# Another order of experts by slot count in a single-core decoder trunk, with gathering groups of three and four

## The chip, the cores and the metric

One Trainium2 chip, of which the kernel uses one core. The metric is the device time of one execution in microseconds (us), the median over runs. In the text PE is TensorE (PEld its weight loads), DVE is VectorE, ACT is ScalarE, POOL is GpSimd and SP is SyncE, which here issues the weight loads.

## The reference, cut to what matters

Two decoder layers on 256 tokens of width 1024. Layer 0 is a state-space mixer and a dense SwiGLU, layer 1 a dilated attention and then a top-2-of-8 mixture of experts, with a LayerNorm behind each. Only the mixture is touched here:

```
logits = x @ w_router
top_v, top_i = lax.top_k(logits, TOP_K)                 # 2 of 8 experts for each token
gates = jax.nn.softmax(top_v, axis=-1)
...
for e in range(N_EXPERTS):
    y = _swiglu(x, w1[e], w3[e], w2[e])                 # (silu(x @ w1) * (x @ w3)) @ w2, inner width 3584
    out = out + gate_full[..., e, None] * y
```

Everything is float32. The weights of one expert are 44.04 MB (42 pieces of 1 MiB).

## The kernel before, in words

**Slots.** An expert computes only the tokens that chose it. They are gathered into a fixed number of slots, 96 or 64 (`CAPS`, L35). `RANKS` (L34) is the order of use: expert 0 comes first whatever its count, and position i of the others takes the expert of rank `RANKS[i]`, where rank 0 is the expert with the most tokens. Ranks 0 to 3 have 96 slots, ranks 4 to 6 have 64. `places()` and `order()` work the ranks out on the chip, and SP loads the seven addresses of the weights into registers. Expert 0 has 96 slots too, but a branch (L1526) takes a path of 64 slots when at most 64 tokens chose it; the trace shows that path (28 of the 56 multiplications of L1453 have 256 columns, the others 384). In what follows e0 to e7 are the positions of use. Before, their slots are 64, 64, 96, 64, 96, 96, 96, 64, with e0 counted as it ran.

**Chunks.** Each expert has 7 chunks of 512 inner columns. A chunk takes six loads of 1 MiB: four for `up` (w1 and w3) and two for `down` (w2). `chunks()` runs on PE, in order of program: the first halves of `up` of chunk n, the transposes (`flip`) of chunk n-1, two pieces of side work (`aside`), `up` again, then `down` of chunk n-1. A 64-slot expert needs one pass over each load, with two column tiles of 64. A 96-slot expert needs a second pass over the same load (`rest` and `down(n, 1)`) with four column tiles of 32. After the last `down` of an expert, L1579 copies its result out of PSUM (`yw`), and the scatter back to the tokens (`scatter`, L1435) runs as side work in the next expert. So the start of L1579 on DVE is used as the border between experts.

**The ring.** All weight loads go through one queue, SP's, into a ring of 17 buffers of 1 MiB (`Stream`). A load is issued in order as soon as the next buffer has been given back (`give`): behind the only pass of a 64-slot expert, behind the second pass of a 96-slot expert. PE waits for a load with its first matmul on it. The order of loads is fixed.

**Gathering.** The tokens of several experts are gathered together (`GROUPS`, L37): `gather(g)` is eight steps, each four matmuls of as many columns as the group has slots, and a copy to `xe`. Group 0 is expert 0. `gather(1)` runs all at once between e0 and e1, with nothing else on PE. `gather(2)` is side work from the second chunk of e2 on, two steps in a chunk. `one_hots` (L1208) makes the matrices that it multiplies by.

Of the kernel before, what the change touches and what calls it, by code (L numbers as in the profile page):

```python
# [30 lines left out]
PIECES = 6 * NJ  # L31


RANKS = (7, 4, 0, 5, 1, 2, 3, 6)  # L34
CAPS = tuple(96 if i == 0 or r < 4 else 64 for i, r in enumerate(RANKS))  # L35

GROUPS = ((0,), (1, 2, 3, 4), (5, 6, 7))  # L37
SLOTS = max(sum(CAPS[i] for i in g) for g in GROUPS)


# [110 lines left out]
def trunk(ctx: ExitStack, tc: tile.TileContext, a, out, dbg=None):  # L151
# [839 lines left out]
    with ExitStack() as e:  # L991
# [212 lines left out]
        def one_hots(g, src=by_i):  # L1204
            c = 0
            for i in GROUPS[g]:
                for t in range(2):
# [114 lines left out]
    OTg = mw.tile([128, 2, 128], F32, name="OTg")  # L1322
    xes = [mw.tile([128, 8, sum(CAPS[i] for i in g)], F32, name=f"xe{g[0]}") for g in GROUPS[1:]]

# [5 lines left out]
    def experts(ws, pas, pyy):  # L1330
        if pas:
            V.tensor_tensor(out=by_i[:, 2:4, :], in0=by_i[:, 2:4, :], in1=cst[:, None, 24:32].to_broadcast([128, 2, 8]), op=S_)
        with ExitStack() as e:
# [18 lines left out]
            def gather(g):  # L1352

                c, x_, o_ = sum(CAPS[i] for i in GROUPS[g]), xes[g], Ob
                nk = 1 if g else 2
# [35 lines left out]
            def up(n, i, b):  # L1391

                ee = n // NJ
                g = [q for q in range(3) if ee in GROUPS[q]][0]
                x_, x0 = xes[g], sum(CAPS[q] for q in GROUPS[g] if q < ee)
                if b == 0:
# [223 lines left out]
def _constants():  # L1620
# [20 lines left out]
    e = np.arange(8)  # L1641
    uni[:, 392:424] = np.concatenate([PIECES * e, 7 - e, RANKS, CAPS])
    ident = np.zeros((128, 160), np.float32)
# [82 lines left out]
```

## Time and profile before

| | us |
|---|---|
| median of 3 runs | 1506.89 (1505.99 to 1507.74) |
| profiled execution, its own time | 1505.6 |
| its span, first to last instruction | 1503.8 |
| PE busy | 1431.1 (95%) |
| DVE busy | 534.7 (36%) |
| ACT busy | 384.0 (26%) |
| expert part, e1 to e7, by L1579 (start of e1's part 750.06, end of e7 1485.83) | 735.8 |

The busy time of PE covers the whole span; matmuls are pipelined, so a busy PE may still wait a little inside. HBM moved 458.31 MB, of which 334 loads of the expert weights of 1 MiB each are listed as one group.

### The profile page before, as it was taken

How to read it: one execution, taken by the hardware profiler on the slowest of the kernel's cores; microseconds unless marked ns; L12 is line 12 of the kernel's file. 1: busy time of each engine (PE TensorE's matmuls, PEld its weight loads, DVE VectorE, ACT ScalarE, POOL GpSimd, SP SyncE). 2: the span in 40 equal slices, each digit the busy share in tenths (PEclk: the TensorE clock that was granted, in tenths of full speed). 3: DMA queues.
4: the chain of work that ended last, by engine and by line, in shares of the span. 5: the costliest groups of instructions: out<-in, count | busy, mean ns of one | idle time of the engine just before them, and what ended most of it. 6: DMA issues, size and time to landing. Idle time of an engine off the chain costs nothing. (4 is left out here: it accounts for less than half of the span.)

```text
span 1503.8 us, 32304 instructions
## 1 busy us (share of the span) xinstructions
PE 1431.1 (95%) x14108; PEld 1040.5 (69%) x14108; DVE 534.7 (36%) x1022; ACT 384.0 (26%) x633; POOL 125.9 (8%) x162
## 2 busy tenths in 40 slices
PE   7869999999999999999998899998999999999996
PEld 6658899998999999865554466654556665666552
DVE  9998745446666655550110110110100100100103
ACT  6535544334554545420110000100000100100100
POOL 0110566001021000001000000000000000000001
PEclk9889999999999999989999999999999999999998
DMA  7007488554445544459999999999999999999995
GB/s 260 7 30 301 174 258 262 192 182 186 148 154 199 180 154 171 172 242 424 425 426 426 426 425 425 425 425 427 425 424 426 417 397 401 363 372 393 406 426 212
DMA packets 68412, 458.31 MB, mean 305 GB/s; under 512 B 9041, under 2 KB 9716, under 8 KB 15780
## 3 DMA queue, kind: packets, MB, share of 16 engines
q1 hardware_dynamic: 62896, 444.68, 73.5%
q0 software_dynamic: 4128, 8.87, 2.2%
q10 hardware_dynamic: 1236, 2.58, 0.5%
q8 instruction: 115, 1.88, 0.5%
q14 instruction: 37, 0.30, 0.1%
HBM read 454.97 MB, written 3.48 MB: 305 GB/s over the span
## 5 line engine op out<-in xcount | busy, mean ns | idle before, releaser
L1384 PE MATMUL a<-raw,xe 128*64 128x256 f32 (+1 forms) x7152 | 514.1, 328 | 8.5 <-DMA raw<-in_moe 7.8
L1384 PEld LDWEIGHTS a<-raw,xe 128*64 128x64 f32 (+1 forms) x7152 | 349.4, 124 | 162.8 <-issue 24.8
L1384 PE MATMUL y<-raw,h 128*32 128x256 f32 (+1 forms) x1792 | 255.7, 488 | 7.0 <-DMA raw<-in_moe 6.0
L1453 DVE TENSOR_TENSOR sl<-sl,a 128x256 f32<-128x256 f32 (+1 forms) x56 | 27.3, 488 | 562.8 <-PE a L1384 562.6
L110 DVE TENSOR_TENSOR sp<-raw,sp 128x2048 fp32r<-128x2048 f32 (+1 forms) x84 | 187.9, 2243 | 98.3 <-ACT sp L109 98.3
L1384 PEld LDWEIGHTS y<-raw,h 128*32 128x32 f32 (+1 forms) x1792 | 89.9, 123 | 151.5 <-issue 118.9
L109 ACT CAST sp<-raw 128x2048 fp32r<-128x2048 f32 (+1 forms) x85 | 154.3, 1823 | 68.7 <-PE ab L928 32.8
L1103 PE MATMUL qkp<-xT,sp 128*128 128x256 f32 x1152 | 153.1, 287 | 0.0
L1451 ACT ACTIVATE sl<-a 128x256 f32<-128x256 f32 (+1 forms) x56 | 24.5, 438 | 501.4 <-PE a L1384 501.3
L1103 PEld LDWEIGHTS qkp<-xT,sp 128*128 128x128 f32 x1152 | 141.9, 191 | 1.9
L928 PE MATMUL ab<-xT,sp 128*128 128x256 f32 x960 | 117.0, 283 | 0.0
L928 PEld LDWEIGHTS ab<-xT,sp 128*128 128x128 f32 x960 | 116.5, 192 | 0.7
L759 POOL TENSOR_TENSOR lr__1387<-lr__1387,mhalf 128x1 f32<-128x1 f32 x8 | 4.5, 568 | 855.4 <-DVE lr__1387 L758 855.4
L972 PE MATMUL pv<-sp,xT 128*128 128x384 f32 x384 | 72.3, 343 | 3.3 <-ACT xT L800 3.3
L972 PEld LDWEIGHTS pv<-sp,xT 128*128 128x128 f32 x384 | 67.4, 192 | 5.0 <-ACT xT L800 3.8
L1413 ACT COPY h<-ht 128x256 f32<-128x256 f32 (+1 forms) x56 | 23.8, 426 | 181.5 <-PE ht L1412 180.4
L916 PE MATMUL facc<-sp,hh 128*128 128x512 f32 x176 | 54.5, 390 | 0.0
L692 PE MATMUL glu<-sp,xT 128*128 128x512 f32 x144 | 36.7, 415 | 4.3 <-DVE sp L110 4.3
L1436 DVE SCALAR_TENSOR_TENSOR xx<-so,by_i,xx 128x512 f32<-128x512 f32 x28 | 19.7, 746 | 57.6 <-PE so L1435 57.6
L474 PE MATMUL pu<-x0T,raw 128*128 128x256 f32 x128 | 30.7, 403 | 8.3 <-DMA raw<-in_w_in 8.3
L692 PEld LDWEIGHTS glu<-sp,xT 128*128 128x128 f32 x144 | 28.7, 201 | 11.7 <-DVE sp L110 5.1
L916 PEld LDWEIGHTS facc<-sp,hh 128*128 128x128 f32 x176 | 32.4, 188 | 6.3
(270 smaller groups left out, 1164.9 us busy)
## 6 DMA issues: line engine op xcount, KB each, us to landing
raw<-in_moe SPq DMA_DIRECT2D x334, 1024.0 KB, 19.4
raw<-in_ffn SPq DMA_DIRECT2D x33, 1024.0 KB, 6.1
raw<-in_qk SPq DMA_DIRECT2D x24, 1024.0 KB, 4.8
raw<-in_wv SPq DMA_DIRECT2D x16, 768.0 KB, 4.4
raw<-in_w_glu SPq DMA_DIRECT2D x8, 1024.0 KB, 4.7
raw<-in_w_o SPq DMA_DIRECT2D x4, 1024.0 KB, 4.7
raw<-in_w_in SPq DMA_DIRECT2D x3, 1024.0 KB, 10.4
skew<-vecs POOLq DMA_DIRECT2D x64, 36.0 KB, 4.1
```

Source lines behind the costliest of these rows:

```text
L109: self.nc.scalar.copy(out=h_, in_=t_)
L110: (eng or self.nc.vector).tensor_tensor(out=l_, in0=t_, in1=h_, op=ALU.subtract)
L474: T.matmul(pu[:, mm].rearrange("p a b -> p (a b)"), lhsT=w[:, k, mm * 128:mm * 128 + 128], rhs=x0T[:, k, :], start=(k == 0 and mm == mms[0 ...
L692: T.matmul(o[t], lhsT=s_, rhs=m_, start=(kk == 0 and i == 0), stop=(kk == 7 and i == 2))
L916: T.matmul(acc[t][n], lhsT=s_, rhs=m_, start=(j == 0 and f == 0 and ip == 0), stop=(j == NFP - 1 and f == 1 and ip == 2))
L928: T.matmul(o[:, f, :], lhsT=s_, rhs=m_, start=(k == 0 and ip == 0), stop=(k == 7 and ip == 2))
L972: T.matmul(ov[t], lhsT=s_, rhs=m_, start=(kk == 0 and ip == 0), stop=(kk == 7 and ip == 2))
L1103: T.matmul(o[:, qk, :], lhsT=s_, rhs=m_, start=(k == 0 and ip == 0), stop=(k == 7 and ip == 2))
L1384: T.matmul(o[n * g:n * g + n, oc:oc + c], lhsT=lhsT, rhs=rhs[:, c * g:c * g + c], start=start, stop=stop, tile_position=(0, n * g), skip_g ...
L1413: A.copy(out=h_[:, 0:q], in_=p_[:, 0:q])
L1451: A.activation(out=sl[:, 0:c], in_=ob[n, 0][:, 0:c], func=ACTF.Silu)
L1453: V.tensor_tensor(out=sl[:, 0:c], in0=sl[:, 0:c], in1=ob[n, 1][:, 0:c], op=M_)
```

## The change

`RANKS` gets another order, so that the slots of e0 to e7 become 64 (96 in its other path), 96, 64, 96, 96, 64, 96, 64, and the groups become e1 to e3 (256 slots) and e4 to e7 (320 slots), where they were e1 to e4 (320) and e5 to e7 (256). Every expert keeps the slots of its rank. The buffers `xe` change sizes with the groups; their sum stays.

```diff
-RANKS = (7, 4, 0, 5, 1, 2, 3, 6)
+RANKS = (7, 0, 4, 1, 2, 5, 3, 6)
 CAPS = tuple(96 if i == 0 or r < 4 else 64 for i, r in enumerate(RANKS))
 
-GROUPS = ((0,), (1, 2, 3, 4), (5, 6, 7))
+GROUPS = ((0,), (1, 2, 3), (4, 5, 6, 7))
 SLOTS = max(sum(CAPS[i] for i in g) for g in GROUPS)
```

## Rows read from the trace of the kernel before

**Rows 1.** The page: rate in 40 slices; two groups of matmuls (idle before, releaser).

```profile
GB/s 260 7 30 301 174 258 262 192 182 186 148 154 199 180 154 171 172 242 424 425 426 426 426 425 425 425 425 427 425 424 426 417 397 401 363 372 393 406 426 212
...
L1384 PE MATMUL a<-raw,xe 128*64 128x256 f32 (+1 forms) x7152 | 514.1, 328 | 8.5 <-DMA raw<-in_moe 7.8
...
L1384 PE MATMUL y<-raw,h 128*32 128x256 f32 (+1 forms) x1792 | 255.7, 488 | 7.0 <-DMA raw<-in_moe 6.0
```

**Rows 2.** Windows from border to border, e1 to e7 (PE, PEld, DVE, ACT, POOL, clock, DMA).

```profile
740.00:850.36 110.36, 97.67 (x692) 53.60 (x692) 11.92 (x26) 10.30 (x25) 0.00 (x0) 0.98 1.01 426
850.36:971.88 121.52, 120.91 (x1715) 77.12 (x1716) 12.61 (x26) 10.30 (x22) 0.00 (x0) 1.00 1.01 425
971.88:1059.33 87.45, 82.66 (x620) 43.49 (x622) 8.58 (x16) 7.48 (x18) 0.00 (x0) 1.00 1.01 426
1059.33:1177.17 117.84, 117.10 (x1683) 73.88 (x1685) 9.08 (x16) 8.69 (x17) 0.00 (x0) 1.00 1.01 425
1177.17:1294.59 117.42, 117.42 (x1715) 73.93 (x1716) 9.93 (x18) 9.42 (x19) 0.00 (x0) 1.00 0.98 400
1294.59:1411.99 117.40, 117.40 (x1715) 73.93 (x1716) 10.36 (x18) 9.79 (x20) 0.00 (x0) 1.00 0.93 379
1411.99:1485.83 73.84, 73.22 (x550) 38.43 (x548) 8.11 (x15) 7.21 (x17) 0.00 (x0) 1.00 0.97 406
```

**Rows 3.** Windows of three other stretches, columns as in rows 2.

```profile
1160.00:1400.00 240.00, 240.00 (x3564) 151.78 (x3564) 19.87 (x34) 19.32 (x39) 0.00 (x0) 1.00 0.96 390
...
800.00:840.00 40.00, 32.70 (x224) 15.74 (x222) 1.26 (x3) 1.51 (x4) 0.00 (x0) 1.00 1.01 426
1411.99:1480.00 68.01, 68.01 (x528) 37.03 (x528) 8.10 (x14) 6.84 (x16) 0.00 (x0) 1.00 1.01 424
```

**Rows 4.** The page's DMA issues: the expert loads (count, KB each, us to landing).

```profile
raw<-in_moe SPq DMA_DIRECT2D x334, 1024.0 KB, 19.4
```

**Rows 5.** Timeline of PE in e1: start, length, instructions, idle before and releaser.

```profile
742.83 6.78 PE L1364 MATMUL gx<-O,xT 128*128 128x320 f32 x32 [2.29 <-issue]
749.54 3.67 PE L1384 MATMUL a<-raw,xe 128*64 128x256 f32 x32
754.40 0.46 PE L1378 MATMUL ot<-idn,Og 128*96 128x128 f32 x2 [1.18 <-DVE Og L1374]
...
755.58 7.13 PE L1384 MATMUL a<-raw,xe 128*64 128x256 f32 x64
...
801.95 1.94 PE L1384 MATMUL y<-raw,h 128*64 128x512 f32 x8 [0.58 <-DMA raw<-in_moe]
...
816.64 1.94 PE L1384 MATMUL y<-raw,h 128*64 128x512 f32 x8 [0.60 <-DMA raw<-in_moe]
...
846.05 1.94 PE L1384 MATMUL y<-raw,h 128*64 128x512 f32 x8 [0.58 <-DMA raw<-in_moe]
```

**Rows 6.** Timeline of DVE: the multiplication that ends `up` of a chunk.

```profile
942.79 0.56 DVE L1453 TENSOR_TENSOR sl<-sl,a 128x384 f32<-128x384 f32 x1 [12.07 <-PE a L1384]
...
960.64 0.55 DVE L1453 TENSOR_TENSOR sl<-sl,a 128x384 f32<-128x384 f32 x1 [12.07 <-PE a L1384]
...
1267.08 0.56 DVE L1453 TENSOR_TENSOR sl<-sl,a 128x384 f32<-128x384 f32 x1 [15.92 <-PE a L1384]
1283.56 0.56 DVE L1453 TENSOR_TENSOR sl<-sl,a 128x384 f32<-128x384 f32 x1 [15.92 <-PE a L1384]
...
1456.15 0.42 DVE L1453 TENSOR_TENSOR sl<-sl,a 128x256 f32<-128x256 f32 x1 [10.44 <-PE a L1384]
1467.01 0.42 DVE L1453 TENSOR_TENSOR sl<-sl,a 128x256 f32<-128x256 f32 x1 [10.44 <-PE a L1384]
```

**Rows 7.** Timeline of PE at the end of e7.

```profile
1474.08 3.67 PE L1384 MATMUL a<-raw,xe 128*64 128x256 f32 x32
...
1482.07 3.65 PE L1384 MATMUL y<-raw,h 128*64 128x512 f32 x16 [0.52 <-ACT h L1413]
```

## The prediction

> **What bounds the kernel now.** I read the page first. Its row of rates shows 424 to 427 GB/s from slice 18 on, where the experts begin, and a dent to 363 in slices 31 to 37 [rows 1]. So the experts run at the rate of the weight loads, except for one late stretch. Then I cut the expert part at its borders [rows 2]: the reader should look at PE's busy time and at the rate in each line, because one of the two always has slack. In e1 and e3 (64 slots) PE is idle for 12.7 and 4.8 us (some 3 of the first around the gathering) and the rate is full: PE starves. In e4 the rate is full and PE is busy for all but 0.7 us. In e5 and e6, the second and third 96-slot experts in a row, PE is busy for all of 117.4 us and the rate falls to 400 and 379: the ring is full and the loads wait for buffers. From 1160 to 1400 PE has no gap at all [rows 3].
>
> The price of the dent: 240 us x (425 - 390) / 425 = 19.8 us of loading lost [rows 3]; by expert, 117.42 x 25/425 = 6.9 in e5 and 117.4 x 46/425 = 12.7 in e6 [rows 2], and 0.2 behind them [rows 3].
>
> One expert is 44.04 MB in 42 loads of 1 MiB [rows 4], so 103.6 us at 425 GB/s, 2.467 us a load. The timeline agrees: where PE starves, the same matmul of the next chunk (six loads on) starts at 801.95 and 816.64, 14.69 us apart [rows 5], 2.45 a load.
>
> PE's own pace: 16.48 us for a 96-slot chunk and 10.86 for a 64-slot one (differences of neighbouring starts, [rows 6]). Six loads arrive in 14.7 to 14.8, so in a 96-slot expert PE falls behind the loads and in a 64-slot one it catches up. What decides is a **backlog**: how far PE stands behind the place where it would starve, in us of loading. At zero PE starves; at the ring's capacity the loads stop.
>
> **The capacity, from before.** e3 ends starved, backlog 0. e4 takes 117.84, adds 14.2. e5 adds 117.4 - 103.6 = 13.8, makes 28.0, but 6.9 was lost, so the ring held 21.1. e6 adds 13.8 and loses 12.7: 22.2. Hence capacity 21.1 to 22.2 (17 buffers are 42 us; the rest is what PE holds and what is on its way). e7 takes PE 73.84 us against its last 38 loads' 93.7, so 22.2 falls to 2.3 at the end. If no load ever waited, the end would come 19.8 + 2.3 = 22.1 us earlier: the most that any order can give, and the sum below is what is left of it.
>
> **The change part by part.** *gather(1)* has 256 columns instead of 320. With 320 it takes 6.78 us [rows 5]. With 256 it is seen only as side work: a chunk with two of its eight steps takes 17.85, without 16.48 [rows 6], so 1.37 x 4 = 5.5. e1 starts 1.3 us earlier. *gather(2)* grows the other way, from 5.5 to about 6.8, inside e2. On PE the two cancel; their place does not.
>
> *Backlog at the start of e1.* Before, PE ate 26 loads (five chunks of `up`, three of `down`) between 749.54 and the first wait at 801.4: 64.1 us of loading in 51.9, so it had started at 12.2 [rows 5]. After: 10.9.
>
> *e1, now 96 slots.* Two first halves of `up`, 7.1; the wait for `ot`, 755.58 - 753.21 = 2.4 [rows 5]; then what a 96-slot expert takes from border to border, 117.4, less the second pass of the `down` before it. That pass is two loads of six of 16.48 - 10.86 = 5.62, so 1.9. Sum 125.0, for 46 loads of 113.5 (the first `up` of e2 is in it): backlog 22.4. Against a capacity of 21.1, which was read when the ring filled from empty, as here, 1.3 is lost.
>
> *e2, now 64 slots with gather(2).* e7 of before took 73.84 with no next expert behind it; the next one's two first halves of `up` add 7.1 and the wait of 0.5 for ACT goes [rows 7]: 80.4, with the gathering 87.2. That gains back 16.4: backlog 4.7. The steps' copies on ACT and DVE hide behind PE (DVE was busy 12.6 of 121.5 us in e2 [rows 2]); uncovered, they would show as PE waiting at the next step, up to 1 us.
>
> *e3, 96 behind 64.* Before's e2 without its gathering, 121.52 - 5.5 = 116.0: plus 12.4, 17.1. *e4, 96 behind 96:* plus 13.8, 30.9: 9.8 lost. *e5, 64:* 80.4, minus 23.2: it runs empty, PE starves 2 us. *e6:* plus 12.4. *e7:* minus 19.9, so PE starves about 7 us, and the kernel ends at the pace of the loads.
>
> Nothing else costs: `one_hots(1)` makes two matrices fewer and `one_hots(2)` two more on an idle DVE (some 0.3 us each if uncovered), the constants are data, every rank keeps its slots, and what follows the last border is untouched (18.0 us of DVE work from 1485.83).
>
> **Sum.** Lost 1.3 + 9.8 = 11.1 where it was 22.1 with the backlog left over: 11.0 us earlier. The rows come from an execution of 1505.6 us (span 1503.8); the median is 1.3 above it. 1506.9 - 11.0 = **1495.9 us**.
>
> Where PE starves, a rule would speak against the change. Rows first: in 800 to 840 PE starves in every load (busy 32.70 of 40) and the granted clock is 1.00, that is 2.4 GHz [rows 3]. The Trainium skill, "TensorE: Matmul & The Clock Gate", section "HAM oscillation — how this bites in real kernels", says that matmuls in short bursts between waits for DMA fall back to the lower clock and each burst starts slow. By the rows the new starving in e5 and e7 costs no clock and the sum stands; by the rule it would be the slower rival below. The trace does not agree with the rule for waits of this length, 0.6 us at most [rows 5].
>
> **Bounds.** No row shows a 96-slot e1, a 64-slot expert with gathering, or the ring filling twice. e1's loss lies between 0 (capacity 22.4) and 5 (its waits at the start twice as long, and nothing overlapped). e4's loss follows from what e2 gives back: 20 if gathering were free and e2 took 83, 12 if it cost twice as much; then 6 to 14. Together 6 to 17, so a gain of 16 to 5: 1491 to 1502.
>
> **Rivals.**
> *The ring never fills again.* If e2 gives back nearly all, only a few us are lost in e4: gain 16 to 20, 1487 to 1491. For it: capacity is known only from experts in a row. Against: e3 and e4 alone add 26.2, more than 21.1. Chance 0.10.
> *It fills early and stays full.* If e1 loses 5 and e2 hardly drains, e4 loses 13.8: gain 3 to 5, 1502 to 1504. For it: e1 starts with a backlog of 10.9. Against: even with the gathering a 64-slot chunk takes 12.6 us against 14.7 of loading. Chance 0.12.
> *The waiting only moves.* PE's work is the same and PE has no gap from 1160 on; what can be won is its starving in e1 and e3 (13.8 us in the matmul groups [rows 1]). If e5 and e7 starve for as long, nothing is won: 1504 to 1508. e7 would have to begin empty; against it, e6 fills 12.4 just before. Chance 0.06.
> *Slower: the clock falls in e7's starving.* At 1.2 GHz a load's matmuls take 3.9 instead of 1.95 us [rows 5], 1.4 more than a load's arrival. Eight loads at that clock eat the gain of 11; the 11 or so that starve would give 16 us, so 1512. Against: the clock in rows 3. Chance 0.06.
> *The forecast:* 0.66.
>
> **The numbers.** A measurement of this kernel can tell 0.2%, 3.0 us, from no change. The forecast and the first two rivals are faster by more than that, 0.88; the third is the same, 0.06; the fourth slower, 0.06. The range that holds 8 in 10 takes the bounds: 1491 to 1502.
>
> **What would show it.** The rate stays at 425 through e1 to within 2 us, and dents once, at e4 and the chunk behind it, by about 10 us of loading. e3's border to border is 116, e4's 117.4, e2's 87, e5's about 82. PE waits for loads at the end of e5 and through the last half of e7, with the clock at 1.00. The prediction is wrong if a dent of more than 4 us stands in e1, if there is none in e4, or if e6 begins with a full ring.

## The result and the profile after

The changed kernel takes 1498.34 us (median of 4 runs, 1497.14 to 1499.36), the kernel before 1506.62 in the runs beside it: 8.3 us less, a ratio of 0.9946 with a 95% interval from 0.9933 to 0.9958. The forecast was 11.0 less, 1495.9, in a range of 1491 to 1502. In a second set of runs the changed kernel took 1499.08 against 1505.91 (0.9952, 0.9940 to 0.9965), 6.8 us less. The profiled execution of the changed kernel is the slowest of its first four (1499.36).

The page's rates first, in the changed kernel; they answer to [rows 1]:

```profile
GB/s 261 7 30 295 169 263 265 197 183 170 168 143 210 181 133 193 175 214 411 425 425 425 406 415 425 425 426 425 425 393 385 388 426 427 425 426 425 424 427 207
...
L1384 PE MATMUL a<-raw,xe 128*64 128x256 f32 (+1 forms) x7152 | 514.3, 328 | 6.4 <-DMA raw<-in_moe 3.4
...
L1384 PE MATMUL y<-raw,h 128*64 128x512 f32 (+1 forms) x1792 | 255.1, 487 | 3.4 <-DMA raw<-in_moe 2.4
```

The one wide dent at slices 31 to 37 has become two: a shallow one (406, 415) at the end of e1, and one of three slices (393, 385, 388) at e4. PE's idle time for loads fell from 13.8 us (7.8 + 6.0) to 5.8 (3.4 + 2.4).

The same windows from border to border as in [rows 2], for the changed kernel (PE, PEld, DVE, ACT, POOL, clock, DMA share, GB/s):

```profile
749.95:875.90 125.95, 123.98 (x1749) 77.73 (x1749) 11.40 (x24) 10.08 (x21) 0.00 (x0) 1.00 1.00 416
875.90:961.70 85.80, 85.80 (x652) 47.96 (x653) 12.40 (x28) 9.19 (x22) 0.00 (x0) 1.00 1.01 426
961.70:1077.78 116.08, 116.08 (x1683) 72.93 (x1685) 9.08 (x15) 8.69 (x17) 0.00 (x0) 1.00 1.01 425
1077.78:1197.50 119.72, 117.97 (x1715) 74.05 (x1717) 10.36 (x19) 9.79 (x20) 0.00 (x0) 1.00 0.95 391
1197.50:1278.58 81.08, 80.65 (x620) 43.36 (x621) 8.59 (x17) 7.48 (x18) 0.00 (x0) 1.00 1.01 426
1278.58:1395.98 117.40, 116.79 (x1683) 73.49 (x1684) 9.50 (x17) 9.07 (x18) 0.00 (x0) 1.00 1.01 425
1395.98:1477.83 81.85, 75.81 (x550) 38.94 (x547) 8.11 (x15) 7.21 (x17) 0.00 (x0) 1.00 0.99 415
```

Read each line by what gives way. e1: the rate, 416, so 125.95 x 9/425 = 2.7 us of loading lost. e2 and e3: neither, PE is busy throughout and the loads run at full rate; this is the backlog moving inside the ring. e4: the rate, 391, so 119.72 x 34/425 = 9.6 lost. e5: PE, by 0.4. e6: PE, by 0.6, but not for a load (last section). e7: PE, idle 6.0 of 81.85, 5.4 of it for loads, at a granted clock of 1.00. The last border came at 1477.83 where it was 1485.83: 8.0 earlier.

### The profile page after: what moved, and what is told of

Same layout as the page of the kernel before. It is cut to its first block, busy times and chain, and to the rows that moved or that the text cites. A ratio compares the mean times of both kernels' runs of the same rounds, so it can differ in the third digit from the quotient of the medians.

```text
span 1497.6 us, 32304 instructions
## 1 busy us (share of the span) xinstructions
PE 1427.2 (95%) x14108; PEld 1038.4 (69%) x14108; DVE 534.2 (36%) x1022; ACT 384.3 (26%) x633; POOL 124.1 (8%) x162
## 5 line engine op out<-in xcount | busy, mean ns | idle before, releaser
L1384 PE MATMUL y<-raw,h 128*64 128x512 f32 (+1 forms) x1792 | 255.1, 487 | 3.4 <-DMA raw<-in_moe 2.4
L1384 PEld LDWEIGHTS y<-raw,h 128*64 128x64 f32 (+1 forms) x1792 | 90.6, 123 | 146.1 <-issue 116.1
L1436 DVE SCALAR_TENSOR_TENSOR xx<-so,by_i,xx 128x512 f32<-128x512 f32 x28 | 19.7, 747 | 55.4 <-PE so L1435 55.4
L1044 ACT ACTIVATE lg<-lg,mx 128x384 f32<-128x384 f32 x32 | 19.7, 617 | 66.0 <-DVE mx L1043 66.0
```

The costliest lines, as they stand in the source:

```text
L1384: T.matmul(o[n * g:n * g + n, oc:oc + c], lhsT=lhsT, rhs=rhs[:, c * g:c * g + c], start=start, stop=stop, tile_position=(0, n * g), skip_g ...
```

## The experiments

The forecast's theory is a **backlog** that wide (96-slot) experts fill and narrow (64-slot) ones drain, against the ring's capacity; loading time is lost whenever the backlog would pass it. The rivals, one or another in each experiment: that only the number of wide experts in a row counts, that the smaller first gathering makes the gain, or that PE's work alone decides.

**Each half alone.** The new order with the old groups:

```diff
-GROUPS = ((0,), (1, 2, 3), (4, 5, 6, 7))
+GROUPS = ((0,), (1, 2, 3, 4), (5, 6, 7))
```

> The new order with the old groups: e1 to e4 gathered together (352 slots here) and e5 to e7 (224 slots). Theory: e1 starts about 2 us later and loses 2 more; e2 has about 2 less to gather, gives back 2 more and e4 loses 2 less: within 1.5 us of the changed kernel, 1498.3. Rival (the smaller first gathering, which nothing hides, gives a good part of the gain): 1500 to 1504.

Measured: 1498.33 us, ratio 0.9947 (0.9933 to 0.9961): the same as the whole change. Two of its windows, e1 and e4:

```profile
750.90:875.93 125.03, 123.57 (x1749) 77.60 (x1749) 11.40 (x23) 9.79 (x20) 0.00 (x0) 1.00 0.99 413
...
1077.19:1196.49 119.30, 117.97 (x1715) 74.03 (x1716) 10.36 (x19) 9.77 (x20) 0.00 (x0) 1.00 0.97 395
```

e1 loses 125.03 x 12/425 = 3.5 instead of 2.7, e4 119.3 x 30/425 = 8.4 instead of 9.6. The groups only move some loss from the one to the other. The old order with the new groups, an edit of the same line in the kernel before:

> The old order with the new groups: e1 to e3 gathered together (224 slots here) and e4 to e7 (352 slots). Theory: the uncovered gathering is 2 us shorter, but e1 has 64 slots and starves, so it only starves longer; e5 and e6 lose what they lost: 1506.6 within 1.5 us. Rival (the smaller first gathering gives a good part of the gain): 1501 to 1504.

Measured: 1506.27 us, ratio 1.0003 (0.9993 to 1.0012). Within these intervals the groups give nothing by themselves, and the order gives the gain.

**The pair of wide experts elsewhere.**

```diff
-RANKS = (7, 0, 4, 1, 2, 5, 3, 6)
+RANKS = (7, 0, 4, 1, 5, 2, 3, 6)
```

> The order of slots for e1 to e7 is 96, 64, 96, 64, 96, 96, 64: the one pair of 96-slot experts comes where the backlog has just been emptied by a 64-slot expert without gathering. Theory (backlog against the ring's capacity): e1 loses about 2.7 us of loading as in the changed kernel, e4 runs empty, e5 adds 12.4 and e6 13.8, which passes the capacity of 21 to 22 by 4 to 5, and e7 ends with a backlog of about 1. That is 8 to 9 lost or left over against 12.4, so 3 to 4 us faster than the changed kernel: about 1494.5. Rival (what counts is only that no three 96-slot experts stand in a row): the same as the changed kernel, 1498.3.

Measured: 1494.63 us (1493.84 to 1496.61), ratio 0.9927 (0.9914 to 0.9941): 3.7 us under the changed kernel's 1498.34. The two intervals overlap a little, but its slowest run is below the fastest of nine of the changed kernel (1497.12). It is the fastest version here that computes all slots. From the border of e4 on:

```profile
1076.03:1165.34 89.31, 82.87 (x620) 43.37 (x621) 8.58 (x16) 7.49 (x18) 0.00 (x0) 1.00 1.01 426
1165.34:1281.42 116.08, 116.08 (x1683) 72.93 (x1685) 9.09 (x16) 8.70 (x17) 0.00 (x0) 1.00 1.01 425
1281.42:1400.20 118.78, 118.08 (x1715) 74.04 (x1716) 10.35 (x19) 9.81 (x20) 0.00 (x0) 1.00 0.98 402
1400.20:1474.05 73.85, 73.23 (x550) 38.49 (x547) 8.10 (x15) 7.22 (x17) 0.00 (x0) 1.00 0.97 406
```

Here e4 (64 slots) does starve, 6.4 us of 89.31, so the pair starts from an empty ring; e5 loses nothing and e6 118.78 x 23/425 = 6.4, where the pair of the changed kernel started from what e2 had left and lost 9.6. Both orders have at most two wide experts in a row, so the rival falls: it matters what stands ahead of the pair. The capacity comes out again too: from empty, 116.08 - 103.6 = 12.5 and 118.78 - 103.6 = 15.2, less the 6.4 lost, is 21.3.

The agreement of the total, 1494.6 with 1494.5, is in part luck. e1 loses 3.0 here (rate 415 from 748.22 to 874.16), so 3.0 + 6.4 = 9.4 us of loading are lost in all, where the changed kernel lost 12.3. From the start of e1 to the last border it takes 725.8 us (748.22 to 1474.05), the changed kernel 727.9: 2.1 less. About one of that may be due to the shorter stops of PE (0.7 in e6, where e4 of the changed kernel has 1.75; last section). The other 1.7 of the 3.7 lie behind the last border, in a stretch that the theory says nothing of (next section).

**The wide ones first.** The same theory should also give a large loss:

```diff
-RANKS = (7, 0, 4, 1, 2, 5, 3, 6)
+RANKS = (7, 0, 1, 2, 3, 4, 5, 6)
```

> The same experts, the four of 96 slots first: 96, 96, 96, 96, 64, 64, 64 for e1 to e7, both groups of 288 slots. Theory (backlog against capacity): e1 fills the ring and loses about 2, e2 adds 13.8 and its gathering 6, all lost, e3 and e4 lose 13.8 each, then e5 empties the ring and e6 and e7 starve at the full rate. Lost about 49 against 22.1 lost or left over in the kernel before: 27 slower, about 1533. Rival (PE's work decides, which is the same in every order): 1500 to 1508.

Measured: 1535.31 us, ratio 1.0190 (1.0175 to 1.0205), 29.4 slower than the kernel before beside it, where 27 was expected. Its windows of e1 to e4, then e6:

```profile
750.43:876.40 125.97, 123.95 (x1749) 77.73 (x1749) 10.98 (x23) 9.43 (x19) 0.00 (x0) 1.00 0.99 413
876.40:999.48 123.08, 122.73 (x1747) 78.32 (x1748) 13.59 (x29) 11.02 (x23) 0.00 (x0) 1.00 0.89 361
999.48:1116.89 117.41, 117.41 (x1715) 73.94 (x1716) 9.94 (x18) 9.42 (x19) 0.00 (x0) 1.00 0.92 373
1116.89:1234.30 117.41, 117.41 (x1715) 73.94 (x1716) 10.36 (x19) 9.79 (x20) 0.00 (x0) 1.00 0.94 380
...
1315.30:1419.76 104.46, 86.12 (x584) 42.63 (x584) 8.16 (x16) 7.13 (x17) 0.00 (x0) 1.00 1.01 426
```

Lost, by the same formula: 3.6 + 18.5 + 14.4 + 12.4 = 48.9, and the narrow experts behind can't win it back: e6 starves through 18 us at full rate. PE's work is that of every other order, so PE's work does not decide.

**The floor.** The changed kernel with one pass per load in e1 to e7:

```diff
-                    if b or CAPS[n // NJ] == 64:
+                    if b or n >= NJ:
                         give(n, i, hf)
...
-                    if b or CAPS[ee] == 64:
+                    if b or n >= NJ:
                         give(n, 2, hf)
...
-                    cap, capp = (CAPS[m // NJ] if 0 <= m < NS and not few else 64 for m in (n, n - 1))
+                    cap, capp = (CAPS[0] if 0 <= m < NJ and not few else 64 for m in (n, n - 1))
...
-        if CAPS[ee] > 64:
+        if ee == 0:
```

> The changed kernel with the second passes of e1 to e7 left out (slots 65 to 96 of the wide experts are not computed). Theory (loads set the floor, and the ring never fills): PE starves in every expert, each takes 103.6 to 104, the rate stays at 425 to the end, and the time is that of the kernel before less its 22.1 us lost or left over: 1484.5, at most 3 off. Rival (PE's work sets the time in a good part of the experts): the four wide experts lose 37 us of work each, so far below that, 1400 to 1470. What the clock does in seven starved experts in a row is also seen: if it falls, the experts take over 104.

Measured: 1483.87 us, ratio 0.9850 (0.9835 to 0.9865). Three of its windows:

```profile
851.14:954.66 103.52, 90.11 (x616) 45.49 (x616) 11.97 (x27) 8.85 (x21) 0.00 (x0) 1.00 1.01 426
954.66:1058.71 104.05, 86.32 (x584) 42.54 (x584) 8.15 (x16) 7.13 (x17) 0.00 (x0) 1.00 1.01 426
...
1370.57:1464.82 94.25, 77.82 (x518) 38.02 (x518) 7.25 (x12) 6.48 (x15) 0.00 (x0) 1.00 0.97 408
```

e2 to e6 take 103.5 to 104.2 us each, whatever PE does in them, and PE idles through 13 to 18 of these at a clock of 1.00. So the loads set the floor. The last border, 1464.82, is 21.0 ahead of the kernel before; by the medians this kernel is 22.0 faster (1505.84 - 1483.87). The forecast worked out 22.1 as the most that an order can give. The 21.0 does not speak against it, because in this execution the loads were behind already ahead of e1, and no full ring makes up for that later. The kernel before, then this one:

```profile
671.00:750.00 79.00, 76.20 (x546) 42.53 (x544) 4.74 (x11) 9.02 (x21) 4.67 (x2) 0.98 0.99 415
```

```profile
671.00:750.00 79.00, 76.07 (x550) 42.27 (x548) 4.55 (x11) 8.94 (x21) 4.67 (x2) 0.98 0.98 409
```

That is 79 x (415 - 409) / 425 = 1.1 us of loading in a stretch that no order touches; with it 21.0 becomes 22.1.

**The ring's size.** Two buffers fewer:

```diff
-        ws.add([p.tile([128, 2048], F32, name=f"raw{i}") for p, r in ((ring5, (11, 12)), (ring6, range(13, 17))) for i in r])
+        ws.add([p.tile([128, 2048], F32, name=f"raw{i}") for p, r in ((ring5, (11, 12)), (ring6, range(13, 15))) for i in r])
```

> The changed kernel with two buffers fewer in the ring (15). Theory (the capacity is that of the ring, so it falls by two loads, 4.9 us): e1 loses 5 more; e2 then runs empty, e3 adds 12.4, e4 13.8 against a capacity of 16 to 17, which loses about 10 as now: about 1503.5. Rival (what limits is something else, such as how many transfers can stand in the queue): 1498.3 as with 17.

Measured: 1506.58 us, ratio 1.0000 (0.9990 to 1.0009): 8 slower than with 17 buffers, so the ring does set the limit, but by 3 more than expected. Its windows of e1, e2 and e4:

```profile
752.57:877.53 124.96, 123.59 (x1749) 77.58 (x1749) 11.40 (x23) 10.11 (x21) 0.00 (x0) 1.00 0.99 408
877.53:965.31 87.78, 86.45 (x652) 47.81 (x653) 12.40 (x28) 9.19 (x22) 0.00 (x0) 1.00 1.01 426
...
1081.39:1200.98 119.59, 117.96 (x1715) 74.03 (x1716) 10.36 (x19) 9.79 (x20) 0.00 (x0) 1.00 0.94 387
```

e1 loses 5.0 and e4 10.7, together 3.4 more than in the changed kernel. The last border comes 8.35 later (1486.18 against 1477.83), so 4.9 more is missing, and it is missing ahead of the experts. The stretch in which SP stands still until the addresses of the experts are known, in the changed kernel and then with 15 buffers:

```profile
640.00:671.00 31.00, 28.04 (x183) 20.14 (x183) 19.53 (x74) 7.55 (x17) 1.69 (x3) 0.83 0.59 239
```

```profile
640.00:671.00 31.00, 28.03 (x183) 20.38 (x183) 19.52 (x74) 7.55 (x17) 1.69 (x3) 0.83 0.43 171
```

31 us x (239 - 171) GB/s is 2.1 MB, two loads, 2 x 2.47 us: in that time the ring can be only as full as it is large. The expectation had left this out. That e1 lost only 2.3 more, and not 5, fits a smaller backlog at its start, which was not measured by itself. e2 ends starved here (three waits for loads, 0.35 to 0.57 us), so e3 and e4 show the capacity of 15 buffers: 116.08 - 103.6 = 12.5 and 119.59 - 103.6 = 16.0, less the 10.7 lost, is 17.8. That is 3.5 under the 21.3 of 17 buffers; the expectation had 16 to 17.

**The second gathering in a wide expert.**

```diff
-                    if j == 1 and ee == 2:
+                    if j == 1 and ee == 3:
```

> The changed kernel with the second gathering as side work of e3 (96 slots) and not of e2 (64 slots). Theory: e2 takes 6.8 less, empties the ring and starves about 2; e3 adds 12.4 + 6.8, e4 13.8 more, so e4 loses about 2 more than now and nothing else moves: about 1500.3. Rival (the gathering costs what it takes wherever it stands, or it is a narrow expert's drain alone that counts): 1498.3 or faster, down to 1492.

Measured: 1501.47 us (1498.98 to 1504.61), ratio 0.9968 (0.9958 to 0.9978), beside the unchanged one's 0.9952 (0.9940 to 0.9965). That is 2.4 slower by the medians; the intervals overlap. Its e2, e3 and e4:

```profile
874.76:956.23 81.47, 80.75 (x620) 43.35 (x621) 8.58 (x16) 7.48 (x18) 0.00 (x0) 1.00 1.01 426
956.23:1078.22 121.99, 121.85 (x1715) 77.56 (x1717) 12.90 (x27) 10.40 (x21) 0.00 (x0) 1.00 1.01 425
1078.22:1197.19 118.97, 117.88 (x1715) 73.83 (x1717) 10.36 (x19) 9.79 (x20) 0.00 (x0) 1.00 0.95 387
```

e2 comes to its end just starving (0.7 idle) and e4 loses 118.97 x 38/425 = 10.6 instead of 9.6. That is the theory's direction. But e1 loses 0.9 less here (rate 419 from 748.80 to 874.76, so 1.8), and the last border comes at 1477.37, where the second profile of the changed kernel has it at 1477.38. So the trace, which is of the fastest of nine runs, shows no loss in sum, and between the theory's 1500.3 and no change at all this experiment does not decide. What falls is the rival's gain down to 1492.

**The same kernel again.**

> The changed kernel once more, unchanged. Theory: 1498.3 within 1. Its last stretch, from the last border to the end, took 19.8 us in the profile of the changed kernel and 18.0 in that of the kernel before. If that belongs to the end at the pace of the loads, it is 19.8 again; if it varies from execution to execution, it may be 18.0.

Measured: 1499.08 us (1497.12 to 1500.44). Its windows repeat those above to 0.4 us, its last border comes at 1477.38 and its span ends at 1497.1: 19.7 us behind the last border again.

## Why the prediction was right, point by point

**The mechanism** held: full ring, backlog, starving, in the places that the forecast named, and the other orders came out as the same count said (the moved gathering left it open, and with 15 buffers 4.9 us came from a stretch ahead of the experts that the count did not cover). *e1 loses a little* (forecast 1.3, measured 2.7), *e4 loses about ten* (9.8, measured 9.6), *e5 just runs empty, e7 starves and the kernel ends at the pace of the loads*: all seen. The borders: e2 85.8 (forecast 87.2), e3 116.1 (116.0), e5 81.1 (about 82), e6 117.4 (116.0). e4 took 119.7 where 117.4 was forecast. One of the prediction's own signs did not come: the rate was to stay at 425 through e1 to within 2 us and to dent once, and it dented twice, by 2.7 in e1, which is still under the 4 that it called wrong.

That e4's loss was met to 0.2 us is luck. e2 gave back 1.4 more than forecast and e4 took 2.3 longer, so by the forecast's own count 9.8 - 1.4 + 2.3 = 10.7 would have been lost; two errors and a capacity known to about 1 us made up for each other. The bounds for e4 were also drawn narrower than the prediction's rows give: with free gathering e2 takes 80.4 and not 83, with gathering at twice its price 94.0, so it would empty the ring or give back only 9.6, and e4 loses 5 to 17, where 6 to 14 was written. The sum of the two stated bounds is 6 to 19, not 6 to 17. The measured 12.3 lies in all of them.

**The size was off by 2.7 us** (8.3 where 11.0 was forecast; 4.2 in the second set). Counted at the last border of the profiled executions it is 8.0, so 3.0 are missing. First, the loads lost: 2.7 + 9.6 = 12.3 instead of 11.1, which is 1.2, nearly all in e1. PE came to the end of e1 2.7 later than forecast, half of it at the start: gather(1) was costed at 5.5 us and took 5.94, and it began 0.8 later than before (743.63 against 742.83 [rows 5]), so that e1 began at 749.50, as before, and not 1.3 us earlier:

```profile
743.63 5.94 PE L1364 MATMUL gx<-O,xT 128*128 128x256 f32 x32 [2.44 <-issue]
749.50 3.67 PE L1384 MATMUL a<-raw,xe 128*64 128x256 f32 x32
```

The other half is e1 itself, 126.4 us from 749.50 to 875.90 where 125.0 was forecast; 0.6 of that is a stop of PE (last section). The loads were 0.9 late there too (next paragraph), so the backlog at the end of e1 would have been 2.7 - 0.9 = 1.8 larger than forecast, and 1.4 more was lost.

Second, the loads were behind ahead of e1, in the part that the order does not touch. The changed kernel, where the kernel before has 415 GB/s in the same window (see "The floor"):

```profile
671.00:750.00 79.00, 76.05 (x554) 42.34 (x552) 4.61 (x12) 8.75 (x21) 4.66 (x2) 0.98 0.99 410
```

That is 79 x (415 - 410) / 425 = 0.9 us. This rate differs from execution to execution without a change there (412 in the second profile of the same kernel, 421 in the late pair), so it is no effect of the new order. But the gain need not have been larger without it: with loads 0.9 earlier, e1 would have had that much more backlog, and by the forecast's count would have lost it again. What is left, 3.0 - 1.2 - 0.9 = 0.9, is not assigned.

The profiled execution shows 6.2 less in its span and not 8.0: the stretch behind the last border is 19.8 us long (1477.83 to 1497.6) and was 18.0. The prediction had put it at no change, so 1.8 us are a cost that it left out. In both the first matmul behind the branch on `over` waits for the branch; the wait in the changed kernel, then in the kernel before:

```profile
  PEq L1589: 2.6, 1
```

```profile
  PEq L1589: 0.8, 1
```

It is not the starving that makes it longer: the kernel with the new groups alone ends with PE busy, as before (73.53 of 74.14 us), and its last stretch is 19.8 too (1484.52 to 1504.3). The late pair has 18.05 (1474.05 to 1492.1). The changed kernel had the longer one in both of its profiles. What differs is where the branch begins on PE's queue, in the changed kernel, then in the kernel before:

```profile
L1589 PEldq COMPARE_BRANCH  x1: 3955/3955/3955, 1476.2 to 1476.2; - x1
```

```profile
L1589 PEldq COMPARE_BRANCH  x1: 3819/3819/3819, 1482.6 to 1482.6; - x1
```

The branch takes 4.0 and 3.8 us, but begins 1.6 us ahead of the last border in the one and 3.2 in the other, so 1.6 more of it stand behind the border. All ten traces fall into these two groups: 3.2 us ahead in the kernel before and in the late pair (last stretch 18.0), 1.6 in the eight others (19.5 to 21.2). Why PE's queue comes to the branch earlier in those two stays open.

**The rivals.** *The ring never fills again*: refuted, it fills twice. *It fills early and stays full*: refuted, e2 and e3 run at 426 and 425. *The waiting only moves*: refuted, PE's idle time for loads fell by 8.0 us (13.8 to 5.8). *The clock falls in e7's starving*: refuted, 1.00 in that window and through the seven starved experts of the kernel with one pass. The section that the prediction cites, the Trainium skill, "TensorE: Matmul & The Clock Gate", section "HAM oscillation — how this bites in real kernels", describes bursts of matmuls that are shorter than the wait for DMA behind them. Here the bursts are 1.95 us and the waits about 0.6, at most 1.4 in the kernel with one pass, so that case did not arise: these runs do not test it, and the prediction's "does not agree" says too much.

## What to carry to other kernels

When one stream of loads feeds work of two speeds, write down the queue: what each piece adds to the backlog or takes from it, and the capacity read from the trace. Loading time is lost only where the sum passes the capacity, so two slow pieces in a row belong behind a fast piece that has already run empty, and not only "in turns"; here that order was 3.7 us faster than the changed kernel with the same work, some 2 of it up to the last border. A kernel that leaves out the slow part shows the floor, and so what any order can still give. Before two profiled executions are compared to a us, look at what they did ahead of the changed part and behind it: here these two differed by 0.9 and 1.8.

## What was not expected

In the changed order PE stops for 0.6 to 1 us inside wide experts with no releaser that the profile names, among others twice in e4:

```profile
1083.83 4.09 PE L1384 MATMUL a<-raw,xe 128*32 128x128 f32 x41 [0.96 <-issue]
...
1102.50 1.74 PE L1384 MATMUL a<-raw,xe 128*32 128x128 f32 x13 [0.79 <-issue]
```

Over the whole kernel such stops before the `a` matmuls are 3.0 us of its 6.4 idle (6.4 - 3.4), four in number, where the kernel before has one, of 0.7 (8.5 - 7.8). They came again in the second profile of the same kernel (e4 119.38 us) and in the new order with the old groups (119.30). PE sets e4's length, so the two make 1.75 of the 2.3 us by which e4 exceeded 117.4. The late pair has one of 0.7 in its e6. Their cause is open.
